# Small weight parts leave GpSimd, and seven half products in both second feed-forward phases

## The chip, the cores and the metric

One core of one Trainium2 chip. The time is device microseconds of one launch. Engines: TensorE (PE), VectorE (DVE), ScalarE (ACT), GpSimd (POOL) and SyncE (SP), which issues most loads.

## The reference

Two layers of a decoder trunk on 544 token columns: one prompt of 512 and eight sequences of four tokens with a paged cache. Each layer is a feed-forward, a mixer (attention beside an S5 state-space branch) and a second feed-forward, each behind an RMS norm with a shift, a scale and a gate computed from a condition. Width 1024, feed-forward width 2816. Cut to what matters here:

```python
def swiglu(h, w_up, w_down):
    a, b = jnp.split(h @ w_up, 2, axis=-1)
    return (jax.nn.silu(a) * b) @ w_down
```

## The kernel before

The residual x stands transposed in SBUF as eight row tiles of 128 x 544; the columns go through PE in two halves of 272. PE multiplies in a rounded 32-bit form (F32R). To keep accuracy every operand is cut in two: `split()` (lines 59 to 67) casts the weight tile `raw` on ACT to a large part `whi` (L63) and subtracts it from `raw` to get the small part `wlo` (L66). `mm3()` makes three matmuls of each product: L154 large by large, L155 large weight by small input, L156 small weight by large input. Before, L66 runs on DVE or on POOL: alternately where `share` is set, on POOL for the early units, always on DVE in `halves()`. The pool `whl` holds eight such tiles, four pairs; `rawp` holds five raw tiles, loaded by SP.

A feed-forward (`ffn()`) goes over 22 units m of 128 hidden columns. A unit multiplies two 1024 x 128 weight tiles (gate and value) with the normed input, 96 matmuls for both column halves, and DVE and ACT make the gate product `mid` (L408, L412 to L414). After a few units a down chunk multiplies the collected `mid` tiles with the down weights, 8 row tiles by 2 halves, and `resid()` adds to x (L366 to L371). `FCH[0]` has three down chunks of 6, 8 and 8 units, `FCH[1]` five of 4, 4, 4, 4 and 6.

With `cross` set, units from m = 3 on go through `seven()`: the gate and value tiles, halved along their rows, and the four blocks of the input (two row halves by two column halves) form a 2 x 2 block product, which seven half products of 12 matmuls give in place of eight: 84 matmuls. For this `crossed()` makes sums of input blocks once a phase, and `halves()` (lines 73 to 93) makes for each unit the sum tile `s`, differences, and four weight operands A, S, B and a half tile. Two of its 512-wide subtractions, L85 and L87, run on POOL. A is used first. Before, only layer 1's second feed-forward has `cross`.

At the end of a phase `close()` does the last four row tiles of the second column half, the norm's sum of the first half (`norm_sum()`, L322 on DVE and L323, one matmul with ones), splits the four weight units that the next phase needs first (`early`), and makes the normed input: `rstd()` (L294 to L301, eight DVE instructions) and `norm_h()` (L348 on DVE, L350 on ACT for the large part, L351 on DVE for the small part). The squares' sums are added up on POOL (L316, L318).

Beside this run fillers, one step at each `tick()`: the modulation vectors (`ada_steps()`: loads, small matmuls L231, a copy L236 on DVE, transposes L240), `s5_setup()` (powers of the state matrix on POOL) and `s5_tables()` (16 blocks; each has four DVE instructions L809 to L812 and eight on POOL, L817 to L825). The order on each engine is fixed when the program is built; every engine works through its own queue in order and waits on semaphores.

Of the kernel before, what the change touches and what calls it, by code (L numbers as in the profile page):

```python
# [7 lines left out]
F32 = mybir.dt.float32  # L8
F32R = mybir.dt.float32r
I32 = mybir.dt.int32  # L10
AF = mybir.ActivationFunctionType
ALU = mybir.AluOpType
# [3 lines left out]
P = 128  # L16
D = 1024
# [10 lines left out]
HK = 512  # L28
# [4 lines left out]
class Net:  # L33
    def __init__(self, ctx, tc, t):
        self.ctx, self.tc, self.nc, self.t = ctx, tc, tc.nc, t
        pool = lambda name, bufs, **k: ctx.enter_context(tc.tile_pool(name=name, bufs=bufs, **k))
        self.cst = pool("cst", 1)
        self.rawp = pool("rawp", 5)
        self.whl = pool("whl", 8)
        self.early, self.pending = [], None  # L40
        self.hp = pool("hp", 8)
        self.fillers = []
        self.xn = 0
        self.share = True
        self.tmp = pool("tmp", 2)
        self.ps = pool("ps", 8, space=PSUM)
        self.nsplit = 0
        self.ps_n = 0

    def psum(self, tag="ps", dt=F32):  # L50
# [5 lines left out]
        self.loaded = self.nc.sync.dma_start(out=r[:, :n], in_=src)  # L56
        return r

    def split(self, r, n, e=None):
        nc = self.nc  # L60
        hi = self.whl.tile([P, 1024], F32R, tag="whl", name="whi")
        lo = self.whl.tile([P, 1024], F32R, tag="whl", name="wlo")
        nc.scalar.copy(hi[:, :n], r[:, :n])  # L63
        e = e or (nc.gpsimd if self.nsplit % 2 and self.share else nc.vector)
        self.nsplit += 1
        e.tensor_sub(lo[:, :n], r[:, :n], hi[:, :n].bitcast(F32))  # L66
        return hi, lo

    def unit(self, src, n):
# [4 lines left out]
    def halves(self, wa, wb):  # L74


        nc = self.nc
        V, E = nc.vector, nc.gpsimd
        ra, rb = self.raw(wa, D), self.raw(wb, D)
        lo, hi = slice(0, HK), slice(HK, D)  # L80
        s = self.sum.tile([P, D], F32, tag="sum", name="sum")
        A = self.split(ra, D, V)
        V.tensor_add(s[:, hi], rb[:, lo], rb[:, hi])
        V.tensor_sub(s[:, lo], s[:, hi], ra[:, lo])
        E.tensor_sub(rb[:, lo], ra[:, lo], rb[:, lo])  # L85
        S = self.split(s, D, V)
        E.tensor_sub(ra[:, hi], ra[:, hi], s[:, lo])  # L87
        B = self.split(rb, D, V)
        h = self.sum.tile([P, HK], F32R, tag="s4h", name="s4h")
        l = self.sum.tile([P, HK], F32R, tag="s4l", name="s4l")  # L90
        nc.scalar.copy(h, ra[:, hi])
        nc.vector.tensor_sub(l, ra[:, hi], h.bitcast(F32))
        return A, S, B, (h, l)

    def crossed(self, pool):
# [295 lines left out]
    def ffn(self, l, j, up, down, pool, hx, spill=None):  # L391
        g = self.mod[l, 3 * j + 2] if (l, 3 * j + 2) in self.mod else None
        nc = self.nc
        mid = {}
        cross = hx is not None
# [19 lines left out]

        def seven(m, mt):

            A, S, B, S4 = self.halves(up[m], up[NFF + m])
            t1, t2, t3, t4 = self.hx
            V = nc.vector  # L420
            new = lambda tag, **k: self.tmp.tile([P, HN], F32, tag=tag, name="u" + tag, **k)
            X, Y, Z = (self.psum() for _ in range(3))
            x, y, z = (p[:, :HN] for p in (X, Y, Z))
            self.prod(Y, A, 0, self.h[0, 0], True)
            p1 = new("sq")
            nc.scalar.copy(p1, y)
            end(0)
            self.prod(Y, S, 0, t2, False)
            q = new(("rr", "na")[m % 2], bufs=1)
            nc.scalar.copy(q, y)  # L430
            end(1)
            self.prod(X, A, HK, self.h[0, 1], True)
            V.tensor_add(p1, x, p1)
            th = open_silu(p1)
            self.tick()
            self.prod(Y, B, 0, t3, False)
            r = new(("acc0", "acc1")[m % 2], bufs=1)
            nc.scalar.copy(r, y)
            self.prod(Z, S, HK, t1, True)
            V.tensor_add(r, z, r)  # L440

            def third():
                self.prod(Y, B, HK, t4, False)
                close_silu(th, Y, mt, 0)
                self.tick()

            def fourth():
                self.prod(Z, S4, 0, self.h[1, 1], False)
                V.tensor_add(q, z, q)
                close_silu(open_silu(q), r, mt, 1)  # L450
                self.tick()

            self.ends = [third, fourth]
# [30 lines left out]
        def do_up(ms):  # L484
            ms = list(ms)
            while ms:
                n = 2 if ms[0] == 0 else 1
                ws = []
                for m in ms[:n]:
                    self.share = l + j > 0 or m >= 8  # L490
                    if m > 2 and cross:
                        mid[m] = pool.tile([P, 2, 2, HN], F32R, tag="mid", name="mid")
                        seven(m, mid[m])
                        continue
                    ws.append((self.unit(up[m], D), self.unit(up[NFF + m], D)))
                    mid[m] = pool.tile([P, 2, 2, HN], F32R, tag="mid", name="mid")
                s = start(ws) if self.head else None
# [54 lines left out]
        while done < NFF:  # L552
            n = min(room - live, NFF - done)
# [9 lines left out]
    def close(self, one):  # L563

        after, first = self.after
        for i in range(4):
            one(4 + i, 1)
            if i == 0:
                with self.tc.high_priority(100):
                    self.norm_sum(0)  # L570
            if i == 1:
                with self.tc.high_priority(100):
                    after(0, 0)
            if first:
                self.early.append(self.split(self.raw(first[i], D), D, self.nc.gpsimd))

        after(0, 1)

        def rest():
            with self.tc.high_priority(100):  # L580
                i = self.norm_sum(1)
                after(1, 0)
                after(1, 1)
            return i

        self.pending = rest
        if not first:
            self.settle()
# [490 lines left out]
    def mixer(self, l):  # L1079
# [5 lines left out]
        with ExitStack() as ctx:  # L1085
            pool = lambda c, name, bufs, **k: c.enter_context(
                tc.tile_pool(name=f"{name}{l}", bufs=bufs, reuse_waits="tile", **k))
            self.share = False
            sm = pool(ctx, "sm", 1)
            q = (sm.tile([P, 8, NSM], F32, tag="qn", name="qn"), sm.tile([P, 2, 8, 8, 4], F32, tag="qr", name="qr"))  # L1090
            cqs = sm.tile([P, 3, NSM], F32, tag="cqs", name="cqs")
# [552 lines left out]
    def run(self, o):  # L1644
# [15 lines left out]
        self.tick(5)  # L1660
        ups = lambda w: [w[m] for m in (0, NFF, 1, NFF + 1)]
        for i, w in enumerate(ups(t["up1"][0])):
            self.early.append(self.split(self.raw(w, D), D, (nc.vector, nc.gpsimd)[i % 2]))
        for hf in range(2):
            self.norm_h(hf, 0, 0, 0)
        sp = tc.alloc_tile_pool(name="s5s0", bufs=1, side="right", reuse_waits="tile")
# [8 lines left out]
        for l in range(DEPTH):  # L1675
            for half in range(2):
# [3 lines left out]
                room = lambda c, name, bufs: c.enter_context(  # L1680
                    tc.tile_pool(name=f"{name}{l}{half}", bufs=bufs, reuse_waits="tile"))
                with ExitStack() as rooms:
                    cross = l * half
                    pool, hx = room(rooms, "fm", NMID[cross]), None
                    if cross:
                        hx, self.sum = room(rooms, "fx", 6), room(rooms, "fs", 1)
                    ft = room(rooms, "ft", 1)
                    self.share = True
                    if half == 0:
                        n = 3 if l == 0 else 1  # L1690
                        self.fillers = self.fillers[:n] + [self.weave(self.fillers[n:], self.s5_tables(l, ft))]
# [3 lines left out]
                        self.ffn(l, 0, t["up1"][l], t["dn1"][l], pool, hx, self.xscr[l])  # L1695
                    else:
                        if l + 1 < DEPTH:
                            self.fillers = [self.weave(self.fillers, self.s5_setup(l + 1, ft))]
                        self.after = (to_h(l + 1, 0), ups(t["up1"][l + 1])) if l + 1 < DEPTH else (self.final, None)
                        self.ffn(l, 2, t["up2"][l], t["dn2"][l], pool, hx)  # L1700
                if half == 0:
# [117 lines left out]
```

## Time and profile before

| | |
|---|---|
| median of 3 runs | 2935.09 us (2934.06 to 2939.82) |
| profiled execution | 2940.74 us, its span 2939.0 us |
| mean granted TensorE clock | 0.981 |
| matmuls L154, L155, L156 in the program | 21572 in all |
| layer 0: first feed-forward, mixer, second feed-forward begin | 30, 494, 1068 us |
| layer 1: the same | 1512, 1947, 2525 us; the end phase at 2914 us |

The starts are those of the first norm sum (L323) of each phase. In the rows below, a stretch's busy time stands beside the number of instructions in brackets; "idle before" is the time for which an engine had nothing to do ahead of the row, with the releaser that ended it. A weight load (PEld) overlaps matmuls. The granted clock is a share of full speed.

### The profile page before, as it was taken

Reading aid. Unit: us, or ns where it says so; the run is one execution under the profiler, and the core shown is the slowest. Engines: PE = TensorE matmul, PEld = TensorE weight load, DVE = VectorE, ACT = ScalarE, POOL = GpSimd, SP = SyncE. Lnnn points to the kernel's source line nnn. Section 1 sums busy time; section 2 is a strip of 40 time slices with the busy share of each in tenths; the row PEclk is TensorE's granted clock in tenths of the full one; section 3 lists DMA queues with packets and bytes.
Section 4 is the critical chain, followed back from the end, with each engine's and each line's share of the span. In section 5 each row is a group of like instructions: output and inputs, shape, how many; then the busy total and the mean of one; then the engine's idle time right before and its main releaser. Section 6 shows DMA issues by size and latency. Waiting matters only on the chain. (4 is left out here: it accounts for less than half of the span.)

```text
span 2939.0 us, 61342 instructions
## 1 busy us (share of the span) xinstructions
PE 2822.0 (96%) x24238; PEld 2643.5 (90%) x24238; DVE 1647.3 (56%) x3217; ACT 945.7 (32%) x1776; POOL 1256.6 (43%) x1461
## 2 busy tenths in 40 slices
PE   6989999999999999999999999999999999899997
PEld 4889999999878889989999999999997789899997
DVE  6384435464675463563453433463747744797776
ACT  3112122234443232122232222233344522344442
POOL 8635434281356258712133561244805551332223
PEclk9999999999999999999999999999999999999998
DMA  7597565637669624693225655236377785132332
GB/s 274 171 314 227 169 182 144 203 132 224 221 217 298 219 82 158 198 318 130 87 74 195 183 174 147 90 107 209 125 247 249 234 266 178 58 95 93 94 94 67
DMA packets 287314, 510.38 MB, mean 174 GB/s; under 512 B 73521, under 2 KB 167090, under 8 KB 287026
## 3 DMA queue, kind: packets, MB, share of 16 engines
q1 hardware_dynamic: 264050, 455.52, 48.5%
q0 software_dynamic: 13760, 42.03, 4.5%
q10 hardware_dynamic: 9216, 8.92, 0.9%
q8 instruction: 190, 3.11, 0.4%
q14 instruction: 98, 0.80, 0.1%
HBM read 452.99 MB, written 61.75 MB: 175 GB/s over the span
## 5 line engine op out<-in xcount | busy, mean ns | idle before, releaser
L154 PE MATMUL ps<-hhi,whi 128*128 128x272 f32 x3320 | 971.8, 296 | 16.4 <-ACT whi L63 12.4
L155 PE MATMUL ps<-hlo,whi 128*128 128x272 f32 x3320 | 964.2, 291 | 13.5 <-DVE hlo L351 12.0
L156 PE MATMUL ps<-hhi,wlo 128*128 128x272 f32 x3320 | 965.0, 292 | 5.4 <-DVE wlo L66 3.6
L63 ACT CAST whi<-raw 128x1024 fp32r<-128x1024 f32 (+2 forms) x416 | 413.0, 994 | 902.5 <-PE ps L155 479.1
L154 PEld LDWEIGHTS ps<-hhi,whi 128*128 128x128 f32 x3320 | 628.9, 191 | 49.1 <-issue 21.4
L155 PEld LDWEIGHTS ps<-hlo,whi 128*128 128x128 f32 x3320 | 635.2, 191 | 18.8 <-DVE hlo L351 13.8
L156 PEld LDWEIGHTS ps<-hhi,wlo 128*128 128x128 f32 x3320 | 632.2, 191 | 8.1 <-DVE wlo L66 4.4
L66 POOL TENSOR_TENSOR wlo<-raw,whi 128x1024 fp32r<-128x1024 f32 (+2 forms) x129 | 288.8, 2239 | 675.2 <-ACT whi L63 593.6
L66 DVE TENSOR_TENSOR wlo<-raw,whi 128x1024 fp32r<-128x1024 f32 (+2 forms) x287 | 350.9, 1223 | 342.6 <-ACT whi L63 333.0
L154 PE MATMUL ps<-mid,whi 128*128 128x272 f32 x1408 | 408.5, 291 | 2.2 <-ACT whi L63 2.2
L156 PE MATMUL ps<-mid,wlo 128*128 128x272 f32 x1408 | 405.9, 289 | 0.0
L155 PE MATMUL ps<-mid,whi 128*128 128x272 f32 x1408 | 404.3, 287 | 0.0
L154 PEld LDWEIGHTS ps<-mid,whi 128*128 128x128 f32 x1408 | 264.2, 188 | 8.3 <-issue 5.1
L155 PEld LDWEIGHTS ps<-mid,whi 128*128 128x128 f32 x1408 | 265.4, 189 | 0.2
L156 PEld LDWEIGHTS ps<-mid,wlo 128*128 128x128 f32 x1408 | 264.7, 188 | 0.8 <-DVE wlo L66 0.4
L1502 POOL DMA_INDIRECT strm<-in_cacheT,idx x128 | 132.3, 1033 | 130.8 <-PE ps L1419 49.3
L414 DVE TENSOR_TENSOR mid<-th,mid 128x272 fp32r<-128x272 f32 x176 | 153.2, 872 | 60.7 <-ACT mid L413 60.3
L412 DVE TENSOR_TENSOR th<-th,ps 128x272 f32<-128x272 f32 x157 | 68.2, 436 | 208.4 <-PE ps L156 202.7
L368 DVE SCALAR_TENSOR_TENSOR x<-ps,mod,x 128x272 f32<-128x272 f32 (+1 forms) x256 | 121.7, 477 | 107.0 <-PE ps L156 106.8
L1502 POOL DMA_INDIRECT strm<-in_cache,idx x128 | 128.5, 1004 | 109.5 <-PE ps L1455 72.3
L413 ACT CAST mid<-th 128x272 fp32r<-128x272 f32 x176 | 73.3, 418 | 255.4 <-DVE th L412 255.2
L154 PE MATMUL ps<-zhi,whi 128*128 128x272 f32 x512 | 152.1, 297 | 0.0
(399 smaller groups left out, 4982.8 us busy)
## 6 DMA issues: line engine op xcount, KB each, us to landing
raw<-in_up SPq DMA_DIRECT2D x176, 512.0 KB
raw<-in_ada_w SPq DMA_DIRECT2D x144, 512.0 KB
raw<-in_w_in SPq DMA_DIRECT2D x60, 512.0 KB
raw<-in_dn SPq DMA_DIRECT2D x48, 512.0 KB
strm<-in_cacheT SPq DMA_DIRECT2D x128, 160.0 KB
s5WW<-w2scr SPq DMA_DIRECT2D x32, 512.0 KB
raw<-in_w_glu SPq DMA_DIRECT2D x32, 512.0 KB
strm<-in_cache SPq DMA_DIRECT2D x128, 128.0 KB
```

The lines of the kernel that those rows point to most:

```text
L63: nc.scalar.copy(hi[:, :n], r[:, :n])
L66: e.tensor_sub(lo[:, :n], r[:, :n], hi[:, :n].bitcast(F32))
L154: nc.tensor.matmul(out, wh[:, s], rh, start=first, stop=False, **more)
L155: nc.tensor.matmul(out, wh[:, s], rl, start=False, stop=False, **more)
L156: nc.tensor.matmul(out, wl[:, s], rh, start=False, stop=last, **more)
L368: nc.vector.scalar_tensor_tensor(xx, ps[:, :np_], g[:, m, 0:1], xx, ALU.mult, ALU.add)
L412: nc.vector.tensor_mul(th, th, pb[:, :HN])
L413: nc.scalar.copy(mt[:, hf, 0], th)
L414: nc.vector.tensor_sub(mt[:, hf, 1], th, mt[:, hf, 0].bitcast(F32))
L1502: self.nc.gpsimd.indirect_dma_start(out=out, out_offset=None, in_=src.rearrange("l n p f -> (l n p) f"), in_offset=bass.IndirectOffsetOnAx ...
```

## The change

Four things, and one size.

1. `split()` no longer alternates. The small part is made on DVE, except where the caller names the weight's place in HBM (`src`): there ACT writes the negated large part into `wlo` and POOL issues a transfer that adds the weight from HBM to it. That is so for two early units at the program's start, all four early units of the five later starts that have them, and for A in `halves()` where `aside` is set: all 19 units of layer 1, every odd m of layer 0. In all 51 units, 29 of them in `halves()`.
2. The two POOL subtractions in `halves()` go to DVE, one with a tile `t` of its own.
3. `cross` holds for layer 0's second feed-forward too: seven products for 19 of its units, five down chunks instead of three, and the sums of `crossed()`.
4. `s5_setup()` of layer 1 works on two halves of its columns, one after the other.
5. POOL's room for transfer descriptors (`dynamic_dma_scratch_size`) is 4096 instead of 8192.

The matmuls fall from 21572 to 21344; POOL's 129 L66 go away, POOL's transfers rise from 284 to 338, DVE's two-operand instructions from 1820 to 2188.

```diff
-        e = e or (nc.gpsimd if self.nsplit % 2 and self.share else nc.vector)
-        self.nsplit += 1
-        e.tensor_sub(lo[:, :n], r[:, :n], hi[:, :n].bitcast(F32))
+        if src is None:
+            nc.vector.tensor_sub(lo[:, :n], r[:, :n], hi[:, :n].bitcast(F32))
+        else:
+            nc.scalar.activation(lo[:, :n], hi[:, :n].bitcast(F32), AF.Copy, scale=-1.0)
+            nc.gpsimd.dma_start(out=lo[:, :n], in_=src, accum_op=ALU.add)
...
-        A = self.split(ra, D, V)
+        t = self.sum.tile([P, HK], F32, tag="dif", name="dif")
+        A = self.split(ra, D, wa if self.aside else None)
...
-        E.tensor_sub(rb[:, lo], ra[:, lo], rb[:, lo])
-        S = self.split(s, D, V)
-        E.tensor_sub(ra[:, hi], ra[:, hi], s[:, lo])
-        B = self.split(rb, D, V)
+        S = self.split(s, D)
+        V.tensor_sub(rb[:, lo], ra[:, lo], rb[:, lo])
+        V.tensor_sub(t, ra[:, hi], s[:, lo])
+        B = self.split(rb, D)
...
-        nc.scalar.copy(h, ra[:, hi])
-        nc.vector.tensor_sub(l, ra[:, hi], h.bitcast(F32))
+        nc.scalar.copy(h, t)
+        V.tensor_sub(l, t, h.bitcast(F32))
...
+            self.aside = l > 0 or m % 2 > 0
             A, S, B, S4 = self.halves(up[m], up[NFF + m])
...
-                self.early.append(self.split(self.raw(first[i], D), D, self.nc.gpsimd))
+                self.early.append(self.split(self.raw(first[i], D), D, first[i]))
...
-            self.early.append(self.split(self.raw(w, D), D, (nc.vector, nc.gpsimd)[i % 2]))
+            self.early.append(self.split(self.raw(w, D), D, w if i % 2 else None))
...
-                    cross = l * half
+                    cross = half
...
-                            self.fillers = [self.weave(self.fillers, self.s5_setup(l + 1, ft))]
+                            self.fillers = [self.weave(self.fillers, self.s5_setup(l + 1, ft, ((1, 2), (0, 1))))]
...
-    nc = bacc.Bacc("TRN2", target_bir_lowering=False, num_devices=1, dynamic_dma_scratch_size=8192)
+    nc = bacc.Bacc("TRN2", target_bir_lowering=False, num_devices=1, dynamic_dma_scratch_size=4096)
```

In the changed kernel the lines from 60 on lie up to four lower: L66 is L65 (DVE), the negation L67 and the transfer L68 are new, L154 to L156 are L157 to L159, L322 and L323 are L325 and L326, L809 to L812 are L812 to L815.

The change moves instructions. Three places.

DVE, from the first norm sum of layer 1's first feed-forward on (`lsq` is the last square, `ny` and `na` are rstd's tiles, `tX` and `tW` table products). Before:

```order
L322 SCALAR_TENSOR_TENSOR lsq<-lsq,acc_18471 128x272
L366 TENSOR_TENSOR rs<-ps,mod_4919 128x32
L368 SCALAR_TENSOR_TENSOR x<-ps,mod_4919,x 128x240
L371 TENSOR_TENSOR x<-x,rs 128x32
L294 TENSOR_SCALAR ny<-ps 128x272
L295 TENSOR_TENSOR na<-ny 128x272
L296 SCALAR_TENSOR_TENSOR na<-na,ps 128x272
L297 SCALAR_TENSOR_TENSOR na<-na 128x272
L298 SCALAR_TENSOR_TENSOR ny<-na,ny 128x272
L299 TENSOR_TENSOR na<-ny 128x272
```

Now:

```order
L325 SCALAR_TENSOR_TENSOR lsq<-lsq,acc_19202 128x272
L813 TENSOR_TENSOR tW<-tX 128x4x64
L814 TENSOR_TENSOR tX<-tF,tB 128x512
L297 TENSOR_SCALAR ny<-ps 128x272
L815 TENSOR_TENSOR tW<-tX 128x4x64
L298 TENSOR_TENSOR na<-ny 128x272
L812 TENSOR_TENSOR tX<-tF,tB 128x512
L299 SCALAR_TENSOR_TENSOR na<-na,ps 128x272
L813 TENSOR_TENSOR tW<-tX 128x4x64
L369 TENSOR_TENSOR rs<-ps,mod_4921 128x32
L371 SCALAR_TENSOR_TENSOR x<-ps,mod_4921,x 128x240
L300 SCALAR_TENSOR_TENSOR na<-na 128x272
```

The table products L812 to L815 stood elsewhere and now stand between the steps of rstd.

PE, around the second norm sum of the same phase (`hhi`, `hlo`: the new input's parts). Before:

```order
L156 MATMUL ps<-hhi,wlo 128x272
L154 MATMUL ps<-hhi,whi 128x272
L155 MATMUL ps<-hlo,whi 128x272
L156 MATMUL ps<-hhi,wlo 128x272
L323 MATMUL ps<-lsq,ones 128x272
L154 MATMUL ps<-hhi,whi 128x272
```

Now:

```order
L157 MATMUL ps<-mid,whi 128x272
L158 MATMUL ps<-mid,whi 128x272
L159 MATMUL ps<-mid,wlo 128x272
L157 MATMUL ps<-hhi,whi 128x272 x4
L326 MATMUL ps<-lsq,ones 128x272
L234 MATMUL ps<-raw,cs 32x256 x13
L158 MATMUL ps<-hlo,whi 128x272
L159 MATMUL ps<-hhi,wlo 128x272
```

Before, 38 matmuls of the new phase stand ahead of the second norm sum; now 4, and behind it 13 of the modulation's (L234).

ACT, in a unit of layer 1's second feed-forward (`sum` is the tile s, `usq` a product copied from PSUM). Before:

```order
L63 CAST whi<-sum 128x1024
L91 CAST s4h<-raw 128x512
L63 CAST whi<-raw 128x1024 x2
L426 COPY usq<-ps 128x272
L63 CAST whi<-sum 128x1024
L408 ACTIVATE th<-usq 128x272
L63 CAST whi<-raw 128x1024
L430 COPY urr<-ps 128x272
```

Now:

```order
L63 CAST whi<-raw 128x1024
L67 ACTIVATE wlo<-whi 128x1024
L63 CAST whi<-sum 128x1024
L63 CAST whi<-raw 128x1024 x2
L67 ACTIVATE wlo<-whi 128x1024
L430 COPY usq<-ps 128x272
L63 CAST whi<-sum 128x1024
L411 ACTIVATE th<-usq 128x272
L63 CAST whi<-raw 128x1024
```

A negation L67 follows the cast of A, ahead of the next unit's copies.

## Rows read from the trace of the kernel before

**Rows 1.** The page's busy times: us, share of the span, instructions of each engine.

```profile
PE 2822.0 (96%) x24238; PEld 2643.5 (90%) x24238; DVE 1647.3 (56%) x3217; ACT 945.7 (32%) x1776; POOL 1256.6 (43%) x1461
```

**Rows 2.** Busy time of each engine by stretch, with granted clock and transfers.

```profile
core 0: us, PE busy (x) PEld busy (x) DVE busy (x) ACT busy (x) POOL busy (x), PEclk, DMA share, GB/s
494.00:524.00 30.00, 25.96 (x176) 24.97 (x175) 29.02 (x58) 10.98 (x21) 15.03 (x14) 0.89 0.28 89
1068.00:1104.00 36.00, 29.45 (x214) 26.66 (x215) 33.23 (x66) 13.85 (x26) 28.61 (x38) 0.91 0.30 90
1120.00:1200.00 80.00, 80.00 (x670) 76.33 (x669) 26.52 (x37) 20.74 (x37) 75.06 (x111) 1.00 0.47 153
1511.70:1541.70 30.00, 26.56 (x194) 25.13 (x196) 28.78 (x57) 11.94 (x24) 12.24 (x7) 0.89 0.24 71
2525.30:2606.00 80.70, 70.46 (x514) 68.08 (x515) 76.80 (x128) 36.50 (x66) 24.57 (x14) 0.96 0.17 53
2660.00:2720.00 60.00, 60.00 (x479) 60.00 (x478) 47.52 (x85) 27.14 (x49) 16.25 (x11) 1.00 0.32 98
```

**Rows 3.** DVE's timeline at the start of layer 1's first feed-forward.

```profile
1512.93 2.65 DVE L295 TENSOR_TENSOR na<-ny 128x272 f32<-128x272 f32 x1
...
1516.56 2.52 DVE L298 SCALAR_TENSOR_TENSOR ny<-na,ny 128x272 f32<-128x272 f32 x1
1519.11 0.44 DVE L299 TENSOR_TENSOR na<-ny 128x272 f32<-128x272 f32 x1
...
1520.89 2.24 DVE L348 SCALAR_TENSOR_TENSOR ht<-x,mod,ny 128x272 f32<-128x272 f32 x4
...
1523.53 2.11 DVE L351 SCALAR_TENSOR_TENSOR hlo<-ht,mod,hhi 128x272 fp32r<-128x272 f32 x1
...
1525.67 1.83 DVE L351 SCALAR_TENSOR_TENSOR hlo<-ht,mod,hhi 128x272 fp32r<-128x272 f32 x3
...
1527.90 2.54 DVE L348 SCALAR_TENSOR_TENSOR ht<-x,mod,ny 128x272 f32<-128x272 f32 x2
...
1530.46 0.90 DVE L348 SCALAR_TENSOR_TENSOR ht<-x,mod,ny 128x272 f32<-128x272 f32 x2
```

**Rows 4.** POOL's timeline in the same stretch, first and last of four.

```profile
1512.88 2.39 POOL L66 TENSOR_TENSOR wlo<-raw,whi 128x1024 fp32r<-128x1024 f32 x1 [5.09 <-ACT whi L63]
...
1527.28 2.45 POOL L66 TENSOR_TENSOR wlo<-raw,whi 128x1024 fp32r<-128x1024 f32 x1
```

**Rows 5.** DVE's timeline in layer 1's second feed-forward.

```profile
2635.20 1.23 DVE L66 TENSOR_TENSOR wlo<-raw,whi 128x1024 fp32r<-128x1024 f32 x1 [0.33 <-ACT whi L63]
...
2639.77 0.68 DVE L92 TENSOR_TENSOR s4l<-raw,s4h 128x512 fp32r<-128x512 f32 x1
```

**Rows 6.** The hole at 1256 us: timelines of DVE and PE, then stretches.

```profile
1253.10 0.69 DVE L809 TENSOR_TENSOR tX<-tF,tB 128x512 f32<-128x512 f32 x1 [0.74 <-DMA tB<-in_b_rows]
1253.82 0.42 DVE L810 TENSOR_TENSOR tW<-tX 128x256 f32<-128x256 f32 x1
...
1256.17 0.69 PE L240 MATMUL ps<-ident,adae 128*128 128x128 f32 x2 [3.62 <-DVE adae L236]
...
1252.00:1263.00 11.00, 7.38 (x40) 7.17 (x39) 6.80 (x16) 0.81 (x2) 0.52 (x2) 0.69 0.95 314
1256.20:1263.00 6.80, 6.80 (x35) 6.80 (x36) 3.52 (x9) 0.43 (x2) 0.00 (x0) 0.60 0.99 347
```

**Rows 7.** Groups of instructions by line and form, POOL's and ACT's.

```profile
L66 POOL TENSOR_TENSOR wlo<-raw,whi 128x1024 fp32r<-128x1024 f32 x101 | 243.8, 2413 | 582.3 <-ACT whi L63 524.9 <-DMA raw<-in_ada_w 45.7 <-DMA raw<-in_up 7.1
...
L85 POOL TENSOR_TENSOR raw<-raw 128x512 f32<-128x512 f32 x19 | 31.2, 1643 | 67.4 <-DVE sum L83 53.8 <-DVE rs L366 13.5
...
L63 ACT CAST whi<-raw 128x1024 fp32r<-128x1024 f32 x340 | 356.5, 1049 | 759.7 <-PE ps L155 435.3 <-DMA raw<-in_up 161.3 <-issue 46.5
```

**Rows 8.** POOL's timeline around a transfer of 256 KB that it issues.

```profile
529.68 0.61 POOL L889 DMA_DIRECT2D s5h<-in_h_scan  x1 [10.94 <-DVE hlo L345]
532.82 1.22 POOL L893 TENSOR_TENSOR s5h<-lam,s5h 128x256 f32<-128x256 f32 x2 [2.52 <-DMA s5h<-in_h_scan]
```

More of the change, by code (lines that the diff above doesn't have):

```diff
@@ L43, in __init__ @@
         self.xn = 0
-        self.share = True
         self.tmp = pool("tmp", 2)
         self.ps = pool("ps", 8, space=PSUM)
-        self.nsplit = 0
         self.ps_n = 0
@@ L57, in raw, with split @@
         return r
-    def split(self, r, n, e=None):
+    def split(self, r, n, src=None):
         nc = self.nc
@@ L77, in halves @@
         nc = self.nc
-        V, E = nc.vector, nc.gpsimd
+        V = nc.vector
         ra, rb = self.raw(wa, D), self.raw(wb, D)
@@ L489, in do_up @@
                 for m in ms[:n]:
-                    self.share = l + j > 0 or m >= 8
                     if m > 2 and cross:
@@ L1087, in mixer @@
                 tc.tile_pool(name=f"{name}{l}", bufs=bufs, reuse_waits="tile", **k))
-            self.share = False
             sm = pool(ctx, "sm", 1)
@@ L1687, in run @@
                     ft = room(rooms, "ft", 1)
-                    self.share = True
                     if half == 0:
```

## The prediction

> **What bounds the kernel now.** I read the page's totals first, then the busy times by stretch, then the timelines of single engines where PE has holes. The totals [rows 1] give PE 96% of the span and no other engine above 56%, so a change pays through the number of matmuls and through the holes in front of PE. In a full stretch PE does 479 matmuls in 60.00 us at a granted clock of 1.00 [rows 2]: 0.1253 us each. That pitch turns every other stretch into a loss: elapsed time less 0.1253 us for each matmul. The starts of the two mixers hold 176 matmuls in 30.00 us each (the first one stands there), a loss of 7.9 us; the start of layer 0's second feed-forward 214 in 36.00, a loss of 9.2; the start of layer 1's, with its sums and half products, 514 in 80.70, a loss of 16.3; the start of layer 1's first feed-forward 194 in 30.00, 13 of them narrow, a loss of about 7 [rows 2].
>
> Why PE waits there stands in DVE's timeline of the last of these [rows 3]. DVE works without a pause on the norm's chain, and the chain sets when the first columns of the new input exist. Some of its instructions take five times as long as their like: L295 2.65 us, where L299, of the same form, takes 0.44; L298 2.52; L351 2.11. Beside them stand four GpSimd L66 of about 2.4 us [rows 4], and the stretched ones each read two operands from SBUF. Against their short likes (L348's is 0.45 each) the excess of the rows is 2.2 + 2.1 + 0.4 + 1.7 + 0.5 + 1.6 = 8.5 us. So four subtractions on GpSimd cost DVE most of their own length, in the one place where DVE sets the pace.
>
> **The change, part by part.** All against the profiled execution, 2940.7 us, which is 5.65 us above the median of the three plain runs.
>
> *Seven products in layer 0.* 19 units drop 12 of 96 matmuls: 228 x 0.1253 = **-28.6 us**. PE was full in the up phases, so this is on the path, if DVE keeps up. For a full unit DVE then has three 1024-wide parts at 1.23, five 512-wide subtractions and sums at 0.68 [rows 5], and three sums from PSUM, two gate products and two L414, 272 wide, at 0.44 as L299 [rows 3]: 3.7 + 3.4 + 3.1 = 10.2 us, against 84 x 0.1253 = 10.5 on PE. A unit whose first part is made aside needs 9.0. The down chunks of four give DVE slack again. With ada copies between, I charge **+3** (0 to 10).
>
> *The hole at 1256.* PE waits 3.62 us for a copy of the modulation, behind table products L809 to L812 on DVE, and then, after that idle stretch, goes on at a granted clock of 0.60, so mostly at the lower of its levels (1.2 of 2.4 GHz); the 11 us hold 40 matmuls, a loss of 6 [rows 6]. In the new order no table product stands in that phase: **-6** (-7 to 0).
>
> *The starts of the mixers.* The four GpSimd subtractions go, and of the early units' small parts only a negation on ACT and a transfer is left. If the 8.5 us of blocking went wholly, PE would wait for the chain's own length, some 3 us of the 7.9. I take -4.5 each, **-9** (-10 to 0). ACT now has four more instructions of 1.05 us [rows 7] between those of the chain, and POOL's four transfer issues wait for them with the norm's sums behind them: **+2** over the four starts (0 to 5).
>
> *Start of layer 0's second feed-forward.* It gets the sums of crossed() and the DVE work of halves(). The nearest row is layer 1's start, which has them: 16.3 lost against 9.2, so +7. The subtractions' 8.5 go, which by itself gives -1.4. But the S5 setup still fills POOL there, 75 of 80 us between 1120 and 1200 [rows 2], now in twice as many, narrower instructions, so I stay near the upper value: **+5.5** (-2 to 13).
>
> *Start of layer 1's second feed-forward.* 8.5 us of blocking go; two POOL subtractions a unit (L85 took 1.64 us, [rows 7]) become two on DVE at 0.68, 5.4 us over the four units of that stretch, and ACT has its negations: **-2** (-8 to 5).
>
> *Start of layer 1's first feed-forward.* Here the order turns against the change. The table products that ran in the phase before now stand between the steps of the norm's chain: 26 of them from the first norm sum to the last small part of the input, 6.5 blocks of twice 0.69 + 0.42 us [rows 6], 14.4 us. The last down chunk has six k-tiles for eight, so the columns that PE still has while it waits are 54 matmuls, not 72: 2.3 us less cover. And PE has only 4 matmuls of the new phase ahead of the second norm sum, which itself waits for DVE. Less the 8.5 of blocking this is +8.3. POOL makes its own halves of the tables behind its transfers, and may hold DVE as its L66 did: **+10** (4 to 18).
>
> *The first of a pair, made aside.* 29 units, 10 in layer 0 and 19 in layer 1, get their first small part by cast (1.05), negation (1.05) and an accumulating transfer. The trace has no accumulating transfer. The nearest row is a plain one of 256 KB from POOL: 3.14 us from the start of its issue to the instruction that used it [rows 8]. Another 256 KB at the 347 GB/s of a full stretch [rows 6] add 0.75: 3.9. If adding means reading a second stream, 512 KB more at that rate make 5.4. So the part is ready 6.3 to 7.8 us after its buffer is free, with 0.3 for the hand-overs. In the new order PE has 56 to 103 matmuls between those points in layer 1, mostly 65 to 76, that is 7.0 us at the least and mostly 8.1 to 9.5. That fits narrowly: **+4** (0 to 58, the upper end being 2 us late each time). DMA has room: a share of 0.32 and 98 GB/s in that phase [rows 2], to which 512 KB in 10.5 us add 50.
>
> On the extra stream there is a rule in the Trainium skill, which speaks against the change: "Collectives: The Full Stack", in "The bandwidth ceiling: the fold count and why AG ≠ RS ≠ AR", puts the halved rate of a reducing transfer down to its two source reads rather than to the addition. By it the slower of my two values holds, and with a plain transfer's price the term would be 0. No run so far shows which.
>
> *The rest.* L66 moves from POOL to DVE in the other phases too: 1.23 us for 2.41 [rows 5, 7], in phases where DVE has slack as in the full stretch, 12.5 of 60 us [rows 2]; nothing, that slack being the cover. Were it gone, each would cost its 1.23. The smaller room for POOL's transfer descriptors would only make a transfer late, which is the last term again.
>
> **Sum.** -28.6 - 6 - 9 + 2 + 5.5 - 2 + 10 + 4 + 3 = -21.1: 2919.6 us for a profiled execution, **2914** for the median.
>
> **Rivals.**
> 1. *Late accumulating transfers: slower.* If the transfer takes 7 us and more instead of 5.4, most asides are late. PE's first product of a unit needs that part, so lateness goes straight to the end: 29 us for every microsecond. For it: the kind of transfer is in no row, and POOL issues it in order, with S5 setup and norm sums ahead of it in layer 0. Against it: the DMA engines are two thirds idle there. At 1 us late past the estimate the saving is gone, at 1.5 us the time is 2914 - 4 + 44 = 2954. It decides from 0.8 us on: 2933.
> 2. *DVE becomes the bound: no change.* Both dear starts come out at their upper ends (+7.5 and +8) and layer 0's up phase, 10.2 of 10.5 us full, loses its 10: 2914 + 7.5 + 8 + 7 = 2936. For it: any blocking by POOL's setup on a unit with 0.3 us of slack. Against it: the blocking instructions with wide operands are gone.
> 3. *The starts are relieved in full: faster still.* Tables on DVE at their lower end (+4), layer 0's start at -1, asides on time, up phase 0: 2914 - 6 - 6.5 - 4 - 3 = 2895. For it: the table products can slip into pauses where the chain waits for ACT. Against it: rows 3 show no pause.
> 4. That the change does not do what it says: the seven products stand in the program, so only their worth is open, and that is rival 2.
>
> **How the numbers follow.** No change is within 0.2%, 2929 to 2941, about what a measurement of this kernel can tell. My forecast, itself 2901 to 2928, has 0.55; rival 1 has 0.18; rival 2 0.13, of which a little is slower; rival 3 0.14. Faster is forecast and rival 3, with a little of the slower two's near ends: 0.70. Same 0.12, slower 0.18. The range goes from just above rival 3's value to rival 1's at 1.5 us late: 2898 to 2955; beyond it lie a late transfer of 2 us and more, and part of rival 3.
>
> **What would show it.** 228 fewer matmuls, and a second feed-forward of layer 0 shorter by 20 to 30 us. No L295, L298, L348 or L351 of over 1 us at the mixers' starts, whose loss falls to 3 to 4 us. At the start of layer 1's first feed-forward PE's loss rises to 15 to 20, with the wait ending on the norm sum or the small part of the input. In layer 1's second feed-forward stretches at 479 matmuls in 60 us speak for transfers on time; waits of PE for the aside's part, ended by a POOL transfer, speak for rival 1. The prediction is wrong if those waits come to over 0.5 us a unit, or if layer 0's up phase has PE waiting for the small parts that DVE makes.

## The result and the profile after

The change made the kernel **slower**: 2959.34 us (median of 5 runs, 2955.06 to 2965.22) against 2935.88; ratio 1.0081, 95% interval 1.0068 to 1.0094. The forecast was 2914, the range ended at 2955. The profiled span grew from 2939.0 to 2957.6 us.

The busy times after, of the page's first part, columns as in [rows 1]:

```profile
PE 2807.5 (95%) x24010; PEld 2618.1 (89%) x24010; DVE 1750.2 (59%) x3618; ACT 1055.9 (36%) x1946; POOL 1022.6 (35%) x1472
```

PE is busy for 14.5 us less and the span is 18.6 us longer: about 33 us more stand in front of it. The 228 matmuls that went would be 28.6 us at 0.1253 us each; the busy time fell by less, in part because others ran at the lower clock (the granted clock over layer 0's second feed-forward is 0.97, it was 0.98). Cut at the first norm sum of each phase, the two traces and the run without asides (below) compare like this, in us:

| | head and first feed-forward, layer 0 | mixer 0 | second feed-forward 0 | first feed-forward 1 | mixer 1 | second feed-forward 1 | end |
|---|---|---|---|---|---|---|---|
| before | 494.0 | 574.1 | 443.6 | 435.7 | 577.9 | 388.6 | 25.1 |
| after | 496.7 | 570.8 | 454.4 | 444.9 | 572.4 | 394.7 | 23.7 |

The phase that lost 228 matmuls is 10.8 us longer. The stretches that answer to [rows 2], then the place of the old hole at 1256 and pieces of layer 0's second feed-forward (in order of time; columns: stretch, length, busy time and count of PE, PEld, DVE, ACT, POOL, granted clock, DMA share, GB/s):

```profile
core 0: us, PE busy (x) PEld busy (x) DVE busy (x) ACT busy (x) POOL busy (x), PEclk, DMA share, GB/s
496.70:526.70 30.00, 25.33 (x182) 24.32 (x182) 23.76 (x62) 14.66 (x25) 8.68 (x14) 0.94 0.66 159
1067.50:1103.50 36.00, 28.67 (x216) 24.93 (x216) 34.52 (x65) 18.46 (x34) 29.68 (x55) 0.95 0.68 156
1130.00:1180.00 50.00, 38.88 (x281) 35.16 (x281) 36.12 (x52) 19.36 (x35) 42.60 (x64) 0.86 0.49 144
1136.25:1140.85 4.60, 4.60 (x20) 4.60 (x21) 1.38 (x2) 0.93 (x2) 4.60 (x14) 0.50 0.17 70
1171.35:1175.00 3.65, 3.65 (x16) 3.65 (x17) 0.07 (x1) 0.68 (x2) 2.54 (x7) 0.50 0.42 157
1245.00:1256.00 11.00, 11.00 (x90) 9.69 (x89) 6.85 (x15) 5.67 (x12) 0.00 (x0) 1.00 0.70 223
1521.90:1551.90 30.00, 24.86 (x160) 21.32 (x161) 25.32 (x64) 10.70 (x18) 4.74 (x6) 0.81 1.01 289
2539.20:2619.90 80.70, 69.34 (x504) 67.50 (x505) 68.81 (x134) 43.80 (x74) 8.65 (x10) 0.92 0.44 102
2674.00:2734.00 60.00, 59.58 (x474) 59.36 (x473) 44.52 (x93) 29.84 (x51) 2.82 (x4) 1.00 0.55 137
```

By 0.1253 us a matmul, the mixer's start loses 7.2 us, where it lost 7.9; the start of layer 0's second feed-forward 8.9 (9.2 before) in its first 36 us, but between 1130 and 1180, where PE had been full before, another 14.8 go. Layer 1's first feed-forward has 160 matmuls in its first 30 us, for 194. In layer 1's second one a full stretch has 474 matmuls, not 479. The hole at 1256 is gone: 11.00 of 11.00.

PE's waits over the whole span, by releaser (total us, times, longest):

```profile
PE ps L159 <- DMA wlo<-in_up: 33.2, 17, 6.1
...
PE ps L326 <- DVE lsq L325: 17.6, 4, 9.1
PE ps L159 <- DMA wlo<-in_w_in: 8.4, 3, 4.3
PE ps L159 <- DVE wlo L65: 7.7, 4, 3.7
```

41.6 us end on an accumulating transfer (`wlo` from `in_up` or `in_w_in`). Before, PE's waits for the small parts of L66 came to 4.0 from DVE and 1.8 from POOL. The same line for the asides alone, in layer 0's second feed-forward and then in layer 1's:

```profile
PE ps L159 <- DMA wlo<-in_up: 18.1, 7, 6.1
PE ps L159 <- DMA wlo<-in_up: 4.1, 6, 1.1
```

That is 22.2 us for 29 asides, or 0.77 each. The waits for the norm sum's last square grew from 13.4 to 17.6.

The two longest holes of the asides, in the timelines of ACT, POOL and PE (start, us, engine, line; idle before and releaser in brackets):

```profile
1117.88 1.06 ACT L67 ACTIVATE wlo<-whi 128x1024 fp32r<-128x1024 f32 x1
...
1130.74 0.90 POOL L68 DMA_DIRECT2D wlo<-in_up  x1
...
1136.25 0.59 PE L159 MATMUL ps<-hhi,wlo 128*128 128x272 f32 x1 [4.49 <-DMA wlo<-in_up]
...
1150.66 1.06 ACT L67 ACTIVATE wlo<-whi 128x1024 fp32r<-128x1024 f32 x1
...
1161.44 2.59 POOL L747 TENSOR_SCALAR s5sq<-s5pw 64x576 f32<-64x576 f32 x1
1164.07 0.95 POOL L761 COPY lam<-s5pw 64x64 f32<-64x64 f32 x2
1165.11 0.73 POOL L712 TENSOR_TENSOR s5pw<-s5pw,s5tp 128x256 f32<-128x256 f32 x1
1165.89 0.97 POOL L68 DMA_DIRECT2D wlo<-in_up  x1
...
1171.35 0.60 PE L159 MATMUL ps<-hhi,wlo 128*128 128x272 f32 x1 [6.05 <-DMA wlo<-in_up]
```

At 1117.88 ACT negates the large part of A of m = 3. Its transfer is issued at 1130.74, 11.8 us after the negation's end, with POOL busy on S5 setup all that time; PE stands for 4.49 us. For m = 5 the negation ends at 1151.72, and the issue comes at 1165.89 behind the powers (L744 to L747, L761, L712): 14.2 us. PE stands 6.05 us, and after each of the two holes it goes on at the lower of its two levels (1.2 of 2.4 GHz): 20 matmuls in the 4.60 us from 1136.25 on and 16 in the 3.65 from 1171.35 on, at a granted clock of 0.50.

And the end of layer 0's second feed-forward, DVE and PE:

```profile
1512.03 0.58 DVE L813 TENSOR_TENSOR tW<-tX 128x256 f32<-128x256 f32 x1
1512.64 1.14 DVE L814 TENSOR_TENSOR tX<-tF,tB 128x512 f32<-128x512 f32 x1
1513.81 1.27 DVE L815 TENSOR_TENSOR tW<-tX 128x256 f32<-128x256 f32 x1
1515.01 0.49 DVE L371 SCALAR_TENSOR_TENSOR x<-ps,mod,x 128x272 f32<-128x272 f32 x1
1515.42 1.09 DVE L812 TENSOR_TENSOR tX<-tF,tB 128x512 f32<-128x512 f32 x1
1516.54 0.86 DVE L813 TENSOR_TENSOR tW<-tX 128x256 f32<-128x256 f32 x1
...
1519.79 1.09 DVE L812 TENSOR_TENSOR tX<-tF,tB 128x512 f32<-128x512 f32 x1 [0.24 <-DMA tB<-in_b_rows]
1520.80 0.99 DVE L325 SCALAR_TENSOR_TENSOR lsq<-lsq,acc 128x272 f32<-128x272 f32 x1
...
1521.94 1.25 PE L326 MATMUL ps<-lsq,ones 128*128 128x272 f32 x2 [9.09 <-DVE lsq L325]
```

The table products L812 to L815 stand not only between the norm's steps but already ahead of the last square (L325), and beside POOL's own tables some take twice their 0.69 and 0.42 us. PE waits 9.09 us for the norm sum, at a place where there was no wait before.

At the first mixer's start, DVE and PE:

```profile
497.91 0.44 DVE L298 TENSOR_TENSOR na<-ny 128x272 f32<-128x272 f32 x1
...
499.33 0.44 DVE L301 SCALAR_TENSOR_TENSOR ny<-na,ny 128x272 f32<-128x272 f32 x1
...
505.03 0.48 DVE L354 SCALAR_TENSOR_TENSOR hlo<-ht,mod,hhi 128x272 fp32r<-128x272 f32 x1
...
512.57 0.42 PE L159 MATMUL ps<-hhi,wlo 128*128 128x272 f32 x1 [4.34 <-DMA wlo<-in_w_in]
```

L298, L301 and L354 are L295, L298 and L351 of [rows 3] at their short durations, as expected. So the blocking of [rows 3] is gone here. In its place PE stands 4.34 us for the transfer of an early part.

### The profile page after: what moved, and what is told of

It is laid out like the page before. It is cut to its first block, busy times and chain, and to the rows that moved or that the text cites. A ratio compares the mean times of both kernels' runs of the same rounds, so it can differ in the third digit from the quotient of the medians.

```text
span 2957.6 us, 61538 instructions
## 1 busy us (share of the span) xinstructions
PE 2807.5 (95%) x24010; PEld 2618.1 (89%) x24010; DVE 1750.2 (59%) x3618; ACT 1055.9 (36%) x1946; POOL 1022.6 (35%) x1472
## 5 line engine op out<-in xcount | busy, mean ns | idle before, releaser
L159 PE MATMUL ps<-hhi,wlo 128*128 128x272 f32 x2864 | 837.0, 295 | 49.5 <-DMA wlo<-in_up 33.2
L157 PE MATMUL ps<-hhi,whi 128*128 128x272 f32 x2864 | 842.1, 298 | 14.3 <-ACT whi L63 7.2
L158 PE MATMUL ps<-hlo,whi 128*128 128x272 f32 x2864 | 833.9, 292 | 5.3 <-DVE hlo L354 3.3
L65 DVE TENSOR_TENSOR wlo<-raw,whi 128x1024 fp32r<-128x1024 f32 (+2 forms) x381 | 434.4, 1141 | 325.6 <-ACT whi L63 313.3
L159 PEld LDWEIGHTS ps<-hhi,wlo 128*128 128x128 f32 x2864 | 547.7, 192 | 59.3 <-DMA wlo<-in_up 37.1
L157 PEld LDWEIGHTS ps<-hhi,whi 128*128 128x128 f32 x2864 | 546.3, 192 | 43.1 <-issue 18.9
L158 PEld LDWEIGHTS ps<-hlo,whi 128*128 128x128 f32 x2864 | 551.3, 193 | 10.4 <-DVE hlo L354 4.3
L157 PE MATMUL ps<-mid,whi 128*128 128x272 f32 x1408 | 408.6, 292 | 0.0
L159 PE MATMUL ps<-mid,wlo 128*128 128x272 f32 x1408 | 406.2, 289 | 0.0
L157 PEld LDWEIGHTS ps<-mid,whi 128*128 128x128 f32 x1408 | 264.7, 188 | 7.4 <-issue 6.8
L159 PEld LDWEIGHTS ps<-mid,wlo 128*128 128x128 f32 x1408 | 265.4, 189 | 0.8 <-DVE mod L247 0.4
L68 POOL DMA_DIRECT2D wlo<-in_up x43 | 38.4, 893 | 625.6 <-ACT wlo L67 440.0
L371 DVE SCALAR_TENSOR_TENSOR x<-ps,mod,x 128x240 f32<-128x240 f32 (+1 forms) x288 | 136.7, 476 | 67.7 <-PE ps L159 65.1
L157 PE MATMUL ps<-hx,whi 128*128 128x272 f32 x608 | 176.0, 291 | 0.0
L158 PE MATMUL ps<-hx,whi 128*128 128x272 f32 x608 | 174.6, 288 | 0.6 <-DVE hx L115 0.6
L159 PE MATMUL ps<-hx,wlo 128*128 128x272 f32 x608 | 174.4, 289 | 0.0
```

The source lines that it names most:

```text
L65: nc.vector.tensor_sub(lo[:, :n], r[:, :n], hi[:, :n].bitcast(F32))
L68: nc.gpsimd.dma_start(out=lo[:, :n], in_=src, accum_op=ALU.add)
L157: nc.tensor.matmul(out, wh[:, s], rh, start=first, stop=False, **more)
L158: nc.tensor.matmul(out, wh[:, s], rl, start=False, stop=False, **more)
L159: nc.tensor.matmul(out, wl[:, s], rh, start=False, stop=last, **more)
L371: nc.vector.scalar_tensor_tensor(xx, ps[:, :np_], g[:, m, 0:1], xx, ALU.mult, ALU.add)
```

## The experiments

They ran on three other chips, on which the kernel before takes 3011 to 3014 us. In the repeated run of the change, on one of them, the two mixers are 45 and 41 us longer, and the feed-forward phases the same to about 1 us. So feed-forward phases are compared across chips, and times by their ratio to the kernel before on the same chip. "Phase 0" is layer 0's second feed-forward, 443.6 us before and 454.4 after.

**The change again, on one of these chips** (no edit).

> The changed kernel itself, beside the other three: it gives the scale of this chip. If its ratio to the kernel before is again 1.006 to 1.010, ratios of the earlier runs can be read against it; its second feed-forward of layer 0 should again take 454 us and its first feed-forward of layer 1 445, whatever the mixers take on this chip.

Ratio 1.0088 (1.0060 to 1.0115); phase 0 453.5, layer 1's first feed-forward 445.9, its second 394.2. So phases and ratios of the other runs can be read against the change's.

**No asides.**

```diff
-            self.aside = l > 0 or m % 2 > 0
+            self.aside = False
```

> The changed kernel, but no first of a pair is made aside: A in halves() gets its small part from VectorE as S and B do; early units keep the accumulating transfer. Theory T (late accumulating transfers make the loss): in the changed kernel's trace PE stands 22 us in all before an aside's small part, 18 of them in layer 0, and each hole of over 3 us is followed by a stretch at the lower clock; without them the time falls by 25 to 30 us, to about 2930 to 2935. Theory D (DVE is the bound in these phases, and PE would wait there whatever made the part): 29 subtractions of 1.23 us come back to DVE, layer 0's up phase fills it, and the time stays at 2955 or rises.

Ratio 0.9970 (0.9959 to 0.9980), 35 us less than the change (1.0088 - 0.9970 of 3012). Phase 0 fell to 427.0 us and layer 1's second feed-forward from 394.7 to 388.4: the ten asides of layer 0 cost 27.4 us, the 19 of layer 1 cost 6.3 (one profile each). PE's waits in phase 0 of this run:

```profile
PE ps L326 <- DVE lsq L325: 7.9, 2, 6.0
PE ps L158 <- DVE hlo L354: 3.3, 1, 3.3
PE ps L159 <- DVE wlo L65: 2.9, 2, 2.0
```

No wait for a transfer is among them, and DVE, with 10 of the 29 more subtractions in this phase, does not take their place: 2.9 us on L65 against 18.6 on transfers, early parts among them. Theory T holds, and more came back than the holes' 22 us, as expected of holes with the lower clock behind them, and with small waits that the count of holes leaves out; D falls.

**Early parts on VectorE.**

```diff
-                self.early.append(self.split(self.raw(first[i], D), D, first[i]))
+                self.early.append(self.split(self.raw(first[i], D), D))
```

> The changed kernel, but the early units of the five phase starts get their small parts from VectorE; asides stay. Theory T: the holes before early parts (15.5 us in all, and the lower clock behind the longest) go, the time falls by some 15 to 20 us, to about 2940 to 2945. Theory D: DVE sets the pace at each start, and four subtractions of 1.23 us more at five starts cost up to 25 us: 2960 to 2985.

Ratio 1.0043 (1.0028 to 1.0059), some 14 us under the change, just short of what T gave; DVE's part in D does not show. Phase 0 450.9, layer 1's first feed-forward 440.7, its second 395.5.

**Both.** The two edits together.

> Both: all small parts on VectorE, no accumulating transfer but the two at the program's start. Theory T: the gains of the two runs before add up, 2905 to 2920. Theory D: DVE carries 49 more subtractions, 60 us of work in the places where it is fullest, and the time is 2960 or more. If the gains do not add, the transfers delay each other.

Ratio 0.9959 (0.9937 to 0.9980). Phase 0 takes 431.0, four more than with early transfers and no asides; layer 1's feed-forwards take 439.8 and 386.1, 4.9 and 2.3 less. By the ratios the gains don't add up (35 and 14 would be 49, measured 39), but their intervals leave room for that much; by the phases, one profile each, early transfers are the better choice in phase 0, where DVE also has `crossed()` at the start, and VectorE is in layer 1's feed-forwards.

**Table products behind the norm.** Layer 1's four table products are queued on VectorE behind the last small part of the new input; `last_h` is that instruction.

```diff
+            with (self.tc.issue_after(self.last_h) if l else ExitStack()):
...
+                nc.vector.tensor_mul(x, F, B)
```

> The changed kernel, with layer 1's table products L812 to L815 queued on VectorE behind the last instruction of the normed input of its first feed-forward. Theory B (the table products between the steps of the norm's chain cost 20 us there: a hole of 9.1 us before the first norm sum and 12 us of loss behind it): the time falls by 12 to 20 us, to 2940 to 2947. Rival: the products delay something else as much (the mixer's loads of the tables, or the weights' small parts), and the time stays within 5 us of 2959.

Ratio 1.0043 (1.0030 to 1.0057), about 13 us under the change. Phase 0 became 4.4 us shorter (449.1), layer 1's first feed-forward 8.1 (437.8), and the wait of 9.09 us fell to 2.8: theory B, at the lower end of its size.

**Layer 0's asides only from m = 7 on.**

```diff
-            self.aside = l > 0 or m % 2 > 0
+            self.aside = l > 0 or (m % 2 > 0 and m > 6)
```

> The changed kernel with layer 0's asides only from m = 7 on: the two at m = 3 and 5, whose transfers stand on GpSimd's queue among S5 setup instructions, go to VectorE. Theory Q (the queue in front of the transfer costs most): holes of 4.5 and 6.1 us and the lower clock behind them go, the phase falls from 454 to about 437 us, and the five later asides still cost about 10. Theory X (the transfer itself is too slow): the later ones cost as much each, and m = 3 and 5 on VectorE gain under 8 us.

Ratio 1.0049 (1.0035 to 1.0064), phase 0 442.5: the two asides behind S5 setup cost 11.9 us, 6 each; the eight later ones, against the 427.0 without any, 15.5, or 1.9 each. That is between the theories: the queue is the dearer part for each aside, but the others have a cost of their own, and six times that of layer 1's (6.3 for 19, 0.33 each). One of the slow ones, the transfers from its issue at 1326.81 until its last packet 9.5 us later (queue: packets, MB, share of 16 engines; then issues):

```profile
q1 hardware_dynamic: 569, 2.11, 65.0%
q0 software_dynamic: 144, 0.52, 28.8%
...
raw<-in_ada_w SPq DMA_DIRECT2D x4, 512.0 KB
raw<-in_up SPq DMA_DIRECT2D x3, 512.0 KB
wlo<-in_up POOLq DMA_DIRECT2D x1, 512.0 KB
```

Beside 512 KB of the small part, q0, four times as much goes to loads on q1, and ada loads stand among them. The two of the eight that had 1.8 and 2.1 MB of other traffic in all beside them took 8.3 and 9.5 us from issue to last packet, the six with 0 to 0.85 MB 5.0 to 6.4. PE's waits for these eight came to 6.8 us of the 15.5.

**No ada loads beside them.**

```diff
-                n = (7, 5, 4, 0)[2 * l + half]
+                n = (12, 0, 4, 0)[2 * l + half]
```

On top of the run before; layer 0's first feed-forward is longer (553 us with the head), so only phase 0 counts.

> As the run with layer 0's asides from m = 7 on, but the five modulation vectors that were computed in layer 0's second feed-forward (40 loads of 512 KB) are computed in its first. Theory L (the transfers queue behind loads): those that took 8 to 10 us from issue to the last packet did so beside 0.5 to 1.1 MB of such loads; now all eight asides take 5 to 6 us, and PE's loss over the phase, 16 us above that without asides, falls to within 5 us of it. Rival: GpSimd's issue or the negation is late, and the loss stays 10 us or more above.

The eight transfers took 5.0 to 6.9 us. PE's loss after 350 us of matmul work in phase 0 (a full matmul counted at 0.1253 us, a narrow one of the modulation at about 0.06) is 29.1 us; it was 42.3 with the ada loads and 26.1 in the run without asides. That is within the 5 us of theory L, though four transfers took longer than the 6 I gave, beside down loads; it hangs on the 0.06, and at 0.068 the distance to the run without asides is 5.7 us and not 3.0. And PE's waits for transfers in the phase did not fall. First the run before, then this one:

```profile
PE ps L159 <- DMA wlo<-in_up: 6.8, 5, 2.1
PE ps L159 <- DMA wlo<-in_up: 7.7, 6, 2.5
```

The wait of 2.5 us is one for an early part, so the eight asides went from 6.8 to 5.3 us, 1.5 less. The 320 narrow matmuls of the five vectors left the phase with the loads, and what PE lost around them is in the 13 us too. So theory L is shown for the length of the transfers; that the loads cost the phase more than these 1.5 us is not shown. This was one run.

**A plain transfer.** The addition is left out.

```diff
-            nc.gpsimd.dma_start(out=lo[:, :n], in_=src, accum_op=ALU.add)
+            nc.gpsimd.dma_start(out=lo[:, :n], in_=src)
```

> The changed kernel with the transfers into the small part not adding: the weight itself is written over the negated large part, so the addition is left out and the small parts hold whole weights. Theory S (adding reads a second stream and so takes longer): a transfer alone takes 3.4 to 4.0 us from issue to last packet instead of 5.0, and layer 1's second feed-forward is 4 to 6 us shorter than the 394 us with adding. Rival: a transfer with conversion issued by GpSimd takes 5 us without the addition too, and nothing changes.

DMA shares over 5.2 us from the issue of one transfer (a digit is 0.13 us), and the software queue's share; first the change (adding), with the tail of a load ahead of it, then this run:

```profile
DMA  9998998512009930697739939699693969917000
...
q0 software_dynamic: 144, 0.52, 63.4%
```

```profile
DMA  0000000004699499699998400000000000000000
...
q0 software_dynamic: 144, 0.52, 32.5%
```

Each has 144 packets and 0.52 MB on q0. Adding, they hold the engines for 63.4% of the stretch and end 5.0 us after the issue; plain, for 32.5%, and end after 3.1. Layer 1's second feed-forward fell to 382.7, not by 4 to 6 but by 12 us, its early parts being earlier too. Theory S holds. The page "Collectives: The Full Stack" of the Trainium skill ("The bandwidth ceiling: the fold count and why AG ≠ RS ≠ AR") says of a collective's reduce step, against a copy, that its two source reads and not the addition halve the rate. The engines' time agrees here (63.4 to 32.5), the time until landing grows less, because some 1.2 to 1.6 us of issue come first in either case. Phase 0 still took 442.1 us, with these waits for transfers:

```profile
PE ps L159 <- DMA wlo<-in_up: 12.3, 2, 8.8
```

The two are those of m = 3 and 5: what the queue costs does not go away. All the other waits for asides, 11.6 us of the change's 22.2, are gone in this one run, in both layers and with the ada loads in place.

**The old split with seven products in layer 0.** The kernel before, with three of the change's edits.

```diff
-                    cross = l * half
+                    cross = half
...
-                            self.fillers = [self.weave(self.fillers, self.s5_setup(l + 1, ft))]
+                            self.fillers = [self.weave(self.fillers, self.s5_setup(l + 1, ft, ((1, 2), (0, 1))))]
...
-    nc = bacc.Bacc("TRN2", target_bir_lowering=False, num_devices=1, dynamic_dma_scratch_size=8192)
+    nc = bacc.Bacc("TRN2", target_bir_lowering=False, num_devices=1, dynamic_dma_scratch_size=4096)
```

> The kernel before with its own split() and halves() (GpSimd makes half of the small parts and two of the four differences), and of the change only the seven products in layer 0, the halved S5 setup and the smaller descriptor room, without which it does not fit. Theory T (the products are worth their matmuls less DVE's longer start, and only the transfers lose): second feed-forward of layer 0 at 425 to 435 us, time 5 to 15 us under the kernel before. Rival P (GpSimd is needed free: its subtractions among the S5 setup are late): that phase at 445 or more, time above the kernel before.

Ratio 1.0088 (1.0064 to 1.0113): no better than the change. Phase 0 takes 456.0, layer 1's first feed-forward 451.8. PE's longest group of waits here:

```profile
PE ps L323 <- DVE lsq L322: 26.3, 6, 14.6
```

14.6 us of it in one piece. My expectation failed and rival P's numbers came: with GpSimd's subtractions the tables' lateness at the phase's end is dearer still. So transfers are not the only way to lose the products' gain; whether DVE's blocking or POOL's own lateness weighs more in this run I did not separate.

**Seven products in layer 1 only.**

```diff
-                    cross = half
+                    cross = l * half
```

> The changed kernel with seven products in layer 1 alone, as before: what is left is who makes the small parts, the halved setup and the smaller room. Layer 0's second feed-forward at 440 to 447 us (its S5 tables back inside it), first feed-forward of layer 1 at 430 to 436, second of layer 1 at 394. If the new way of making small parts is a gain by itself outside the asides: 5 to 10 us under the kernel before, ratio 0.997 to 0.9985. If the early transfers and layer 1's asides eat that: ratio 1.000 to 1.003.

Ratio 1.0020 (1.0009 to 1.0031). Phase 0 takes 434.0 us, under the 440 that I expected at the least, and 9.6 less than before without a matmul less (the hole at 1256 and the blocking at the start are gone, and no aside is in it); layer 1's second feed-forward takes 397.6, 9 more. What the new small parts gain in one phase the transfers take back in the other. The halved setup and the smaller descriptor room are in this run as well, so they do not make phase 0 longer.

**The best of these.** No asides, tables behind the norm, early parts by transfer at phase 0's start alone.

```diff
-            self.aside = l > 0 or m % 2 > 0
+            self.aside = False
...
-                self.early.append(self.split(self.raw(first[i], D), D, first[i]))
+                self.early.append(self.split(self.raw(first[i], D), D, first[i] if self.far else None))
```

`far` is true in layer 0's mixer; the table edit is the one above.

> The changed kernel with no asides, table products behind the norm's chain, early small parts on VectorE except at the start of layer 0's second feed-forward, where they stay transfers. From the phases of the runs so far: that phase 422 to 427 us, first feed-forward of layer 1 433 to 438, second of layer 1 386: 15 to 25 us under the kernel before, ratio 0.992 to 0.995. If asides, early transfers and tables hide each other, the phases stay at 427, 440 and 386 and the ratio at 0.996.

Ratio **0.9918** (0.9891 to 0.9946): 25 us under the kernel before and 51 under the change. Phase 0 418.5, better than forecast, layer 1's feed-forwards 438.0 and 386.8. PE's waits in phase 0:

```profile
PE ps L326 <- DVE lsq L325: 4.0, 2, 2.2
PE ps L158 <- DVE hlo L354: 3.3, 1, 3.3
PE ps L159 <- DVE wlo L65: 1.5, 2, 1.3
```

The wait of 9.09 us for the last square at the phase's end is down to 2.2; the other of the two, 1.8, is at its start.

## Why the prediction was wrong

*Seven products, -28.6:* the matmuls went, and without asides and with the tables out of the way phase 0 is 25.1 us shorter, where this term and the three of the next item give -26.1. But not all of it is the products': with the new small parts and eight products the phase already falls to 434.0. Against that run they gave 15.5 us in the best run, and without the move of the tables 7.0 (427.0), which the next phase lost again: 444.7 for 435.0. So on their own the products are worth about half of their matmuls here, and that only once the tables are moved.

*Layer 0's up phase, +3, its start, +5.5, the hole at 1256, -6:* right in sum. PE's loss over 375 us of work in phase 0, counted as above, is 26.2 us in the run without asides and 26.1 before, the hole's share of it being 7. The single sizes were not measured.

*The first of a pair, made aside, +4:* this step failed; it cost 27.4 + 6.3 = 33.7 us. PE's waits came to 0.77 us a unit, above the 0.5 that was to show the prediction wrong. The transfer's own price, estimated at 5.4 us, was nearly right: 4.9 to 5.1 alone. What I left out is what stands around it. The chain was priced as if POOL were free: the 5.4 us count from the issue, which for m = 3 and 5 came 11.8 and 14.2 us after the negation. POOL's 75 of 80 busy us stood in [rows 2], and rival 1 named it; I let the DMA's slack answer for POOL's. And the chain of 6.3 to 7.8 us was set against 7.0 at the least, in layer 1 alone; for layer 0 I gave no such count, and there was no room for a transfer that takes longer than alone. "DMA has room" was read in layer 1's second feed-forward, a share of 0.32; in layer 0's, beside ada loads, transfers took 8 to 10 us. So rival 1 is what happened, in two parts. Of the 22.2 us that PE waited for asides, 10.5 stand behind GpSimd's queue; the other 11.6 go when the addition is left out, so they come of the longer, adding transfer in a chain without slack. The ada loads' share in them is small where it was measured, 1.5 us. How the rest of the 33.7 us, beyond the waits themselves, divides between the lower clock behind the holes and the later norm was not followed.

*Table products in layer 1's first feed-forward, +10:* mechanism right, size too small. That phase grew by 9.2 us, and the phase before ends in the 9.1 us wait, which I did not count: blocks ahead of the norm sum lie on its path too. Moving them gave back some 13 us.

*The mixers' starts, -9 and +2:* the blocking went, as said, but the start of the first lost 7.2 us against 7.9. I had priced the early transfers at a negation's length; there they land 4 to 8 us after their issue, beside each other and the loads, and PE waits for them instead. The mixers are 3.3 and 5.5 us shorter as a whole; where, I did not follow. That their sum of 8.8 lies near the forecast's 7 is luck, since it did not come from the start where I put it.

*Layer 1's second feed-forward, -2:* 394.7 against 388.6, and 388.4 without asides: the start gave nothing.

## What to carry to other kernels

An operation moved to a transfer that a compute engine issues waited here in that engine's queue first, and the transfer itself took longer with the addition and with loads in flight; price it from the end of its input to landing, with the busiest stretch's queue and traffic, not the quietest's. Work that PE waits for belongs on an engine with slack at that place, and which engine that is can differ from phase to phase of one kernel. When a new arrangement shifts unrelated work, look for it ahead of the norm sum as well as behind it. And to price one part of a change that has several, run it against the other parts, not only against the kernel before: 9.6 of phase 0's 25.1 us came without the products.

## What the runs showed of the hardware that I had not expected

An accumulating transfer of 512 KB holds the DMA engines about twice as long as a plain one (63.4% against 32.5% of a 5.2 us stretch) and lands after 5.0 us instead of 3.1. With 1.8 to 2.2 MB of other traffic beside it, it stretches to 8 to 10 us, which agrees with the Trainium skill, "DMA: Bandwidth & Descriptors", "Issuing engines are not separate DMA queues": transfers of all issuers interleave on the same engines. And a hole costs PE more than its length: between 1130 and 1180, where two holes take 10.5 us in all, PE loses 14.8, since after each it goes on at the lower of its two levels (1.2 of 2.4 GHz), for 4.6 and 3.65 us; the granted clock of the whole stretch is 0.86.
